# 32 of the 384 dense tokens of a PEER block take their first products from gathered rows of u

## The chip, the cores and the metric

The program runs on one core of one Trainium2 chip. The metric is device time in microseconds (us) of one execution; lower is better. Everything is fp32, and the large products are each split into three fp32r matmuls (a high and a low part of both operands, without low times low).

## The reference

One encoder layer over 512 tokens of width 1024: a norm, one input projection, attention and an HGRN2 recurrence side by side, a merge, then the part that matters here, PEER retrieval over 16384 one-neuron experts, and last a gated input embedding. The PEER part, cut:

```python
q = (ht @ w_q).reshape(T, 8, 2, 128)
s = einsum('thpc,hpnc->thpn', q, sub_keys)       # scores of 128 row keys and 128 column keys
v1, i1 = top_k(s[:, :, 0], 16);  v2, i2 = top_k(s[:, :, 1], 16)
top_s, pos = top_k(all 256 sums v1 + v2, 16)     # 8 heads x 16 = 128 slots for each token
idx = i1 * 128 + i2 of the chosen;  g = softmax(top_s)
a = einsum('thkd,td->thk', u[idx], x);  w = gelu(a) * g
out = einsum('thk,thkd->td', w, v[idx])
```

## The kernel before

The 512 tokens stand in four blocks of 128. Block 0 (tokens 0 to 127) is **gathered**: for each of its 128 slots one row of u per token comes by an indirect DMA that GpSimd issues (`slot_u`, tile `gu`, 128 rows of 4 KB), VectorE multiplies it with `h2n` and sums it into one column of `aa` (L889); after gelu and the gate (`slot_w`) a row of v follows (`slot_v`, tile `gv`), which VectorE adds into `acc` (L898).

The other 384 tokens (blocks 1 to 3, `TD`) are **dense**: all 16384 experts are computed for them, in 128 chunks of 128 experts. For a chunk `dense_a` loads u (`u_raw`), splits it (`u_h` on ScalarE, `u_l` on VectorE, L139 and L140), and TensorE makes `pa` with 24 matmuls (8 slices of the width, 3 products each, L134 to L136) of 384 columns; ScalarE writes gelu of it to `ge`. The gate table G, which is zero but for the 128 slots of a token, is built in blocks of 32 tokens (`build`, 4 for each token block, 12 in all): one-hot rows `gE` on VectorE, `gR` on ScalarE, a matmul `pg` for each token, and a store of the block to DRAM (`gdram`). For a chunk `w_prep` loads its v rows (`v_raw`, split into `v_h` and `v_l`) and every fourth time a piece of G (`gchg`), multiplies `ge` by G (L1002), and splits the product (`w_h`, `w_l`). Then 18 matmuls of 512 columns add to `po` (3 token blocks, 2 halves, 3 products).

This gives three stages after the query products end at 606 us. **Stage A** (to 1016.7 us, where the first `po` matmul starts): the top-16 choice of each block (`sel`) and the building of G, and beside it the dense chunks at a pace of one for every `APACE` units of a hand-set cost. G is not yet there, so `ge` of the first `SP` chunks is parked in DRAM (`adram`) and read back later (`ges`); `PRE` buffers hold `ge` of the others. Gathers of u start when the cost passes `GSTART` and go on at `GPACE`, from cost 135 on at `GPACE` + `GP2`. The whole cost of the units is 161.4 in both kernels. **Stage B**, 128 iterations `it`: `w_prep`, a fresh dense chunk where one is due, 18 `po` matmuls, and some gathers of u and v; the last `LASTN` = 4 iterations run token block by token block. At `it` = `IT1` = 118 the buffers of the u side are given up, and the embedding part loads its operands (the residual `x`, `pr`) and makes `pj`. **The tail**: residual, norm (`norm_T1`, transposes `pt_n`), and 16 gates of 24 matmuls each (`gate`, tile `pg`, 256 columns).

Each engine takes its instructions in the order in which a scheduler wrote them; the SyncE queue issues all loads and stores but the gathers, also in order, and waits there for a free buffer. The indirect gathers stand in GpSimd's queue. There are 4 `gu` and 4 `gv` buffers, 3 `v_raw`, 3 `u_raw`, 4 each of `v_h`, `v_l`, `w_h`, `w_l` and `ges`.

Of the kernel before, what the change touches and what calls it, by code (L numbers as in the profile page):

```python
# [8 lines left out]
F32 = mybir.dt.float32  # L9
# [19 lines left out]
C_ID, C_IOTA, C_COS, C_SIN, C_RST = 0, 128, 256, 384, 512  # L29
# [19 lines left out]
PRE = 8  # L49
SP = 62  # L50
TQ = 8
APACE = 2.6
# [7 lines left out]
IT1 = 118  # L60
WLAG = 4
# [6 lines left out]
G0 = 8  # L68
# [17 lines left out]
def const_arrays():  # L86
    c = np.zeros((128, C_END), np.float32)
# [18 lines left out]
    return c, m  # L106
# [19 lines left out]
def body(nc, tc, I, out, taps=None, stop=99):  # L126
# [17 lines left out]
    with contextlib.ExitStack() as top:  # L144
        glob = top.enter_context(tc.tile_pool(name="glob", bufs=1))
        cst = glob.tile([128, C_END], F32, name="cst")
# [49 lines left out]
        if True:  # L196
# [4 lines left out]
            hT_l = fp.tile([128, ND, T], F32R, name="hT_l")  # L201
            ysp = [[fp.tile([128, 4, T], F32R, name=f"{nm}{p}") for p in "hl"] for nm in "oy"]
# [11 lines left out]
            with tc.tile_pool(name="n1", side="right", bufs=1) as n1:  # L214
# [4 lines left out]
                DM.dma_start(cst[:, 0:C_COS], I["cst"][:, 0:C_COS])  # L219
# [7 lines left out]
                DM.dma_start(cst[:, C_COS:C_END], I["cst"][:, C_COS:C_END])  # L227
# [105 lines left out]
            def hgrn_head(h):  # L333
# [5 lines left out]
                V.tensor_tensor_scan(SC.rearrange(fl), cst[:, C_RST:C_END], LF.rearrange(fl), 0.0, OP.mult, OP.add)  # L339
# [144 lines left out]
            for tb in range(NT):  # L484
                for (src, dst, H, o, gg) in ((aq[:, tb, :], qr, 8, 0, qn_g), (akv[:, tb, 0:128], kr, 2, 8, kn_g)):
# [7 lines left out]
                    co, si = [cst[:, off + 32 * tb:off + 32 * tb + 32].rearrange("p (a i) -> p a i", a=2)[:, None]  # L493
# [159 lines left out]
        v8s = [pp.tile([128, 16, 16], F32, name=f"v8_{tb}") for tb in range(NT)]  # L653
        i8s = [pp.tile([128, 16, 16], U32, name=f"i8_{tb}") for tb in range(NT)]
        with s5:
# [49 lines left out]
            ul_st = contextlib.ExitStack()  # L705
            up = [ul_st.enter_context(tc.tile_pool(name="ustr0", side="left", **LR))]
# [50 lines left out]
def peer(nc, tc, I, out, xd, cst, gains, norm_T1, rstd_of, split, mm3, tap, stop, pp, ha, la, h2n, v8s, i8s, st, top,  # L757
# [8 lines left out]
    if True:  # L766
# [83 lines left out]
        def build(kp, bp, ps, tb, i_f, g_o):  # L850
# [3 lines left out]
            tij = kp.tile([128, 2, 128], F32, name="tij", tag="tij")  # L854
            S.activation(tij, pt[:, 0:2, :], AF.Copy)
            gr = kp.tile([128, 128], F32, name="gr", tag="gr")
            S.activation(gr, pt[:, 2, :], AF.Copy)
            for b in range(128 // GB):
# [59 lines left out]
        with s7:  # L918
# [42 lines left out]
            for u in units():  # L961
# [4 lines left out]
                if cost > GSTART:  # L966
                    gathers((cost - GSTART) * GPACE + max(0.0, cost - GS2) * GP2, None)
# [7 lines left out]

        vp = ys.enter_context(tc.tile_pool(name="vstr", side="right", bufs=2, reuse_waits="tile"))
# [4 lines left out]
        N0 = na  # L981
        def w_prep(it):
            c = it
# [12 lines left out]
            if spilled:  # L996
                ge = vp.tile([128, TD], F32, name="ges", tag="ges", bufs=B_GE)
                DM.dma_start(ge, ad[spidx[c]])
# [18 lines left out]
        for it in range(128):  # L1017
# [9 lines left out]
            if it < IT1:  # L1027
                if it >= G0:
                    gathers(GW + (it + 1 - G0) * (128 + WLAG - GW) / (IT1 - UEND - G0), VLEAD + (it + 1 - G0) * 128 / (IT1 - G0), ops[0], ops[5])
            if it == IT1:  # L1030
                gathers(999, 999, ops[0], ops[5])
# [8 lines left out]
                with tc.tile_pool(name="ple1a", side="left", **LR) as pa:  # L1040
# [7 lines left out]
                    for n in range(2):  # L1048
# [6 lines left out]
                        for tb in range(NT):  # L1055
                            sl = slice(tb * 128, (tb + 1) * 128)
                            pj = ps1.tile([128, 512], F32, name="pjp", tag="p1")
                            for k in range(2):
                                mm3(pj, ph[:, k, sl], pl[:, k, sl], jh[:, k, :], jl[:, k, :], k == 0, k == 1)
                            S.activation(PJ[tb][:, 512 * n:512 * n + 512], pj, AF.Copy)  # L1060
                V.tensor_tensor(X[0], X[0], acc, op=OP.add)
# [27 lines left out]
                norm_T1(pe2[0], ps1, "p1", X[0], 2, h3h, h3l, "n3", 0, B_XN)  # L1089
                gate(0, 0, *wg0, ps1, "p1")  # L1090
        for tb in range(3):
# [17 lines left out]
def layouts(a):  # L1109
    f = np.ascontiguousarray  # L1110
    c, m = const_arrays()
# [8 lines left out]
    for lo, hi, n in W_IN_TILES:  # L1120
# [24 lines left out]
        "cmask": m,  # L1145
    }
# [17 lines left out]
```

## Time and profile before

| | us |
|---|---|
| median of 3 runs (1858.29 to 1859.44) | 1858.76 |
| the profiled execution, own time | 1863.17 |
| its span in the trace | 1861.4 |
| TensorE busy | 1803.0 (97%) |
| VectorE busy | 1403.1 (75%) |
| ScalarE busy | 902.2 (48%) |
| GpSimd busy | 352.2 (19%) |

The span is what the trace's clock shows from the first to the last instruction. Busy time of TensorE counts matmuls whose ends are modelled and overlap, so what one matmul takes in a stream is read from the starts of two that follow each other. The granted clock is at its full level (2.4 GHz) in nearly all slices.

### The profile page before, as it was taken

The numbers are of one execution on the slowest core, as the hardware profiler recorded it, in microseconds if no ns is written. First come the engines' busy times: TensorE is split into PE (matmuls) and PEld (weight loads), VectorE is DVE, ScalarE is ACT, GpSimd is POOL, SyncE is SP. The second block draws the span as 40 slices with busy tenths as digits, with TensorE's granted clock in tenths as the row PEclk, the third lists the DMA queues.
The fourth block names the chain that finished last, engine by engine and source line by source line (L and its number), as shares of the span: only waits on it lengthen the run. The fifth ranks groups of instructions, "written<-read, shape, count | busy, mean of one in ns | idle before, by whom it ended". The sixth has DMA issues, their size and how long they took to land.

```text
span 1861.4 us, 27255 instructions
## 1 busy us (share of the span) xinstructions
PE 1803.0 (97%) x9989; PEld 1612.1 (87%) x9989; DVE 1403.1 (75%) x2844; ACT 902.2 (48%) x1561; POOL 352.2 (19%) x260
## 2 busy tenths in 40 slices
PE   6999999999999899998999999999999999999998
PEld 5997878888888899998999888888888888888888
DVE  3689776636599999997764888787777778766564
ACT  5745656542433557875696433333333333333442
POOL 0000000000000033333300244344343334321000
PEclk9999999999999999999999999999999999999999
DMA  4212100323321488887857999999999999987612
GB/s 163 83 46 80 58 13 12 122 92 126 146 82 56 142 315 305 298 300 280 329 186 260 359 360 352 316 344 320 336 328 320 314 335 325 312 268 219 208 60 88
DMA packets 162805, 402.95 MB, mean 216 GB/s; under 512 B 13552, under 2 KB 80880, under 8 KB 161008
## 3 DMA queue, kind: packets, MB, share of 16 engines
q1 hardware_dynamic: 125808, 266.98, 41.9%
q0 software_dynamic: 36864, 134.23, 20.2%
q8 instruction: 78, 1.28, 0.3%
q14 instruction: 55, 0.45, 0.1%
HBM read 359.62 MB, written 41.55 MB: 216 GB/s over the span
## 4 chain that ended last, share of the span: by engine, by line
PE 79%; DVE 10%; DMA 4%; ACT 3%; issue 2%; POOL 0%; SPq 0%; ACTq 0%; POOLq 0%; DVEq 0%
PE po L136 9%; PE po L135 9%; PE po L134 9%; PE pa L136 6%; PE pa L135 6%; PE pa L134 6%; PE pT L135 3%; PE pT L134 3%; PE pT L136 3%; PE pg L872 3%; DMA gdram<-gs 2%; PE poa L566 2%; PE pq L135 2%; PE pq L134 2%; PE pq L136 2%
## 5 line engine op out<-in xcount | busy, mean ns | idle before, releaser
L883 POOL DMA_INDIRECT gu<-in_peer_u_dram,idxg x128 | 196.6, 1536 | 1170.5 <-DVE cd L808 646.0
L136 PE MATMUL pa<-ha,u_l 128*128 128x384 f32 x1024 | 348.1, 340 | 11.9 <-DVE u_l L140 11.9
L134 PE MATMUL pa<-ha,u_h 128*128 128x384 f32 x1024 | 349.7, 342 | 1.8 <-ACT u_h L139 1.8
L135 PE MATMUL pa<-la,u_h 128*128 128x384 f32 x1024 | 346.9, 339 | 0.0
L136 PE MATMUL po<-v_h,w_l 128*128 128x512 f32 x768 | 299.9, 391 | 0.1
L135 PE MATMUL po<-v_l,w_h 128*128 128x512 f32 x768 | 300.0, 391 | 0.0
L134 PE MATMUL po<-v_h,w_h 128*128 128x512 f32 x768 | 298.8, 389 | 0.8 <-ACT w_h L139 0.8
L139 ACT ACTIVATE u_h<-u_raw 128x1024 fp32r<-128x1024 f32 x128 | 135.4, 1057 | 214.9 <-PE pa L135 114.0
L136 PEld LDWEIGHTS pa<-ha,u_l 128*128 128x128 f32 x1024 | 193.8, 189 | 14.8 <-DVE u_l L140 14.6
L140 DVE TENSOR_TENSOR u_l<-u_raw,u_h 128x1024 fp32r<-128x1024 f32 x128 | 156.3, 1221 | 63.2 <-ACT u_h L139 63.2
L134 PEld LDWEIGHTS pa<-ha,u_h 128*128 128x128 f32 x1024 | 194.0, 189 | 5.0 <-ACT u_h L139 2.6
L135 PEld LDWEIGHTS pa<-la,u_h 128*128 128x128 f32 x1024 | 193.8, 189 | 2.4
L883 POOL DMA_INDIRECT gv<-in_peer_v_dram,idxg x128 | 155.3, 1213 | 184.1 <-DVE acc L898 161.2
L995 DVE TENSOR_TENSOR v_l<-v_raw,v_h 128x1024 fp32r<-128x1024 f32 x128 | 156.5, 1223 | 39.3 <-ACT v_h L994 38.6
L136 PEld LDWEIGHTS po<-v_h,w_l 128*128 128x128 f32 x768 | 144.1, 188 | 30.7 <-DVE w_l L140 0.7
L134 PEld LDWEIGHTS po<-v_h,w_h 128*128 128x128 f32 x768 | 144.2, 188 | 29.6 <-ACT w_h L139 1.1
L135 PEld LDWEIGHTS po<-v_l,w_h 128*128 128x128 f32 x768 | 144.1, 188 | 28.8
L889 DVE SCALAR_TENSOR_TENSOR gu<-gu,h2n 128x1024 f32<-128x1024 f32 x128 | 155.5, 1219 | 13.4 <-DMA gu<-in_peer_u_dram,idxg 13.4
L898 DVE SCALAR_TENSOR_TENSOR acc<-gv,aa,acc 128x1024 f32<-128x1024 f32 x128 | 164.1, 1282 | 0.4 <-DMA gv<-in_peer_v_dram,idxg 0.2
L994 ACT ACTIVATE v_h<-v_raw 128x1024 fp32r<-128x1024 f32 x128 | 134.2, 1049 | 44.0 <-PE po L136 27.9
L867 ACT ACTIVATE gR<-gE,gr 128x128 f32<-128x128 f32 x384 | 122.2, 394 | 33.1 <-DVE gE L864 32.9
L864 DVE TENSOR_TENSOR gE<-cst,tij 128x2048 f32<-128x2048 f32 x48 | 109.3, 2287 | 17.0 <-PE pg L872 17.0
(321 smaller groups left out, 3341.3 us busy)
## 6 DMA issues: line engine op xcount, KB each, us to landing
u_raw<-in_u_t_dram SPq DMA_DIRECT2D x128, 512.0 KB
v_raw<-in_peer_v_dram SPq DMA_DIRECT2D x128, 512.0 KB
gdram<-gs SPq DMA_DIRECT2D x12, 2048.0 KB
gchg<-gdram SPq DMA_DIRECT2D x32, 768.0 KB
w_raw<-in_w_in_dram SPq DMA_DIRECT2D x42, 512.0 KB
adram<-ge SPq DMA_DIRECT2D x62, 192.0 KB
ges<-adram SPq DMA_DIRECT2D x62, 192.0 KB
wq_raw<-in_peer_wq_dram SPq DMA_DIRECT2D x16, 512.0 KB
```

What stands on the lines that cost most here:

```text
L134: PE.matmul(ps, lh, rh, start=first, stop=False)
L135: PE.matmul(ps, lh, rl, start=False, stop=False)
L136: PE.matmul(ps, ll, rh, start=False, stop=last)
L139: ins = S.activation(hi, raw, AF.Copy)
L140: V.tensor_tensor(lo, raw, hi.bitcast(F32), op=OP.subtract)
L864: V.tensor_tensor(EE, iota[:, None, None, :].to_broadcast([128, 2, TQ, 128]), tij[:, :, t0:t0 + TQ, None].to_broadcast([128, 2, TQ, 128]), ...
L867: S.activation(RR[:, t, :], EE[:, 1, t, :], AF.Copy, scale=gr[:, t0 + t:t0 + t + 1])
L883: G.indirect_dma_start(out=t, out_offset=None, in_=src, in_offset=bass.IndirectOffsetOnAxis(ap=idxg[:, k:k + 1], axis=0))
L889: V.scalar_tensor_tensor(t, t, 1.0, h2n, op0=OP.mult, op1=OP.mult, accum_out=aa[:, k:k + 1])
L898: V.scalar_tensor_tensor(acc, t, aa[:, k:k + 1], acc, op0=OP.mult, op1=OP.add)
L994: S.activation(vh, vr, AF.Copy)
L995: vi.append(V.tensor_tensor(vl, vr, vh.bitcast(F32), op=OP.subtract))
```

## The change

Tokens 128 to 159, the first 32 of the dense ones (`RC` = 32), no longer go through `pa`: a chunk's 24 matmuls have 352 columns, and `ge` holds ones in the first 32. Their first products come from rows of u, laid out anew: 32 tokens times 128 slots are 32 gathers of 128 rows, with 4 groups of 32 slots on the partitions. `rows_h` makes the tokens' vectors for this layout (`hC`), `rows_idx` the indices and gates, `row_u` gathers and multiplies, and `rows_w` puts gelu times gate into `gr`, from which the first block of G is then built, last of all blocks instead of first. Since `ge` is one there, the G table carries the finished weights.

Besides: block 1 is chosen before block 0; `SP` goes from 62 to 66, `PRE` from 8 to 7, `APACE` from 2.6 to 2.44; the paced number of u gathers now counts the 32 new ones first. In stage B the u gathers spread to `it` = 118 (before: 110), those of v to 128 (before: 118), from a pool of their own that outlives the u side; the rest of block 0 (adding `acc`, norm, first gate) moves from `it` = 118 to behind the first token block's last matmuls. The read-back of `ges` is issued ahead of `gchg` and `v_raw`, and `pj` is made at `it` = 123. Some constants and the top-8 lists move to other pools.

```diff
-PRE = 8
-SP = 62
+RC = 32
+PRE = 7
+SP = 66
-APACE = 2.6
+APACE = 2.44
+VEND = 128
 def dense_a(c):
-                mm3(pa, uh[:, e], ul[:, e], ha[:, k, NG:T], la[:, k, NG:T], k == 0, k == ND - 1)
+                mm3(pa[:, RC:], uh[:, e], ul[:, e], ha[:, k, NG + RC:T], la[:, k, NG + RC:T], k == 0, k == ND - 1)
-                S.activation(ge, pa, AF.Gelu_apprx_tanh)
+                S.activation(ge[:, RC:], pa[:, RC:], AF.Gelu_apprx_tanh)
+                S.activation(ge[:, 0:RC], ones, AF.Copy)
+            def rows_h():
+                hs = kp.tile([128, D], F32, name="hs")
+                for dst in (hs, hC):
+                    for half in range(2):
+                        pt = ps.tile([128, 128, 4], F32, name="pg", tag="pg").rearrange("p i t -> p (i t)")
+                        if dst is hs:
+                            for j in range(4):
+                                k = 4 * half + j
+                                for n, h in enumerate((ha, la)):
+                                    PE.matmul(pt[:, j * 128:(j + 1) * 128], h[:, k, NG:NG + 128].bitcast(F32), ident, ...)
+                        else:
+                            PE.matmul(pt, csel[:, 0, :], hs[:, 512 * half:512 * half + 512], start=True, stop=True)
+                        S.activation(dst[:, 512 * half:512 * half + 512], pt, AF.Copy)
+            def rows_idx(i_f, g_o):
+                V.scalar_tensor_tensor(x, i_f[:, 0, :], 128.0, i_f[:, 1, :], op0=OP.mult, op1=OP.add)
+                PE.matmul(pt[:, 0, :], csel[:, 0, :], x, start=True, stop=True)
+                PE.matmul(pt[:, 1, :], csel[:, 0, :], g_o, start=True, stop=True)
...
+            def row_u(k):
+                t = gather(un, k, "gu", idxC)
+                V.scalar_tensor_tensor(t, t, 1.0, hC, op0=OP.mult, op1=OP.mult, accum_out=aC[:, k:k + 1])
+            def rows_w(gr):
+                S.activation(aC, aC, AF.Gelu_apprx_tanh)
+                V.tensor_tensor(aC, aC, gC, op=OP.mult)
...
+                PE.matmul(pt[:, 0, 0:RC], Z, csel[:, 2, 0:RC], start=True, stop=True)
+                S.activation(gr[:, 0:RC], pt[:, 0, 0:RC], AF.Copy)
             def units():
-                yield from sel(0)
-                yield from sel(1)
+                rows_h()
+                yield from sel(TB0)
+                rows_idx(*sels[TB0])
+                yield from sel(0)
                 for tb in (1, 2, 3):
-                    gens = [build(kp, bp, ps, tb, *sels[tb])]
+                    gens = [build(bp, ps, tb, *tg, range(1 if tb == TB0 else 0, 128 // GB))]
...
+                rows_w(first[1])
+                yield from build(bp, ps, TB0, *first, [0])
                 if cost > GSTART:
-                    gathers((cost - GSTART) * GPACE + max(0.0, cost - GS2) * GP2, None)
+                    want = int((cost - GSTART) * GPACE + max(0.0, cost - GS2) * GP2)
+                    while rows["ok"] and rows["n"] < min(RC, want):
+                        row_u(rows["n"])
+                        rows["n"] += 1
+                    gathers(want - RC, None)
-            if it < IT1:
-                if it >= G0:
-                    gathers(GW + (it + 1 - G0) * (128 + WLAG - GW) / (IT1 - UEND - G0), VLEAD + (it + 1 - G0) * 128 / (IT1 - G0), ops[0], ops[5])
+            if it >= G0:
+                gathers(999 if it >= IT1 else GW + (it + 1 - G0) * (128 + WLAG - GW) / (IT1 - G0), (it + 1 - G0) * 128 / (VEND - G0), ops[0], ops[5])
             if it == IT1:
-                gathers(999, 999, ops[0], ops[5])
                 ul_st.close()
```

In the queue of GpSimd, before, the gathers of u of block 0 (`idxg`) come first, with a few of v between them, and those of v follow:

```order
L883 DMA gu<-in_peer_u_dram,idxg 128x1024 x4
L883 DMA gv<-in_peer_v_dram,idxg 128x1024
L883 DMA gu<-in_peer_u_dram,idxg 128x1024 x4
L883 DMA gv<-in_peer_v_dram,idxg 128x1024 x3
L883 DMA gu<-in_peer_u_dram,idxg 128x1024 x55
L883 DMA gv<-in_peer_v_dram,idxg 128x1024 x2
```

At the same place of the changed kernel the 32 gathers of the new rows (`idxC`) lead:

```order
L902 DMA gu<-in_peer_u_dram,idxC 128x1024 x32
L902 DMA gu<-in_peer_u_dram,idxg 128x1024 x29
L902 DMA gv<-in_peer_v_dram,idxg 128x1024 x4
L902 DMA gu<-in_peer_u_dram,idxg 128x1024
L902 DMA gv<-in_peer_v_dram,idxg 128x1024
```

Before the first gather of v is used, block 0 has thus some 29 rows of u where it had some 63; the missing ones move into stage B.

On VectorE, before, from the split of v of `it` = 12 on, what stage B does for two iterations (`ges` and `ge` are multiplied by G, `gu` and `acc` are gather steps):

```order
L995 TENSOR_TENSOR v_l<-v_raw,v_h 128x1024
L1002 TENSOR_TENSOR ges<-ges,gchg 128x384
L889 SCALAR_TENSOR_TENSOR gu,aa<-gu,h2n 128x1024
L995 TENSOR_TENSOR v_l<-v_raw,v_h 128x1024 x2
L1002 TENSOR_TENSOR ges<-ges,gchg 128x384
L140 TENSOR_TENSOR u_l<-u_raw,u_h 128x1024
L1002 TENSOR_TENSOR ge<-ge,gchg 128x384
L889 SCALAR_TENSOR_TENSOR gu,aa<-gu,h2n 128x1024
L140 TENSOR_TENSOR w_l<-ge,w_h 128x384
L898 SCALAR_TENSOR_TENSOR acc<-gv,aa,acc 128x1024
L140 TENSOR_TENSOR w_l<-ges,w_h 128x384
```

The same place of the changed kernel:

```order
L1094 TENSOR_TENSOR v_l<-v_raw,v_h 128x1024
L1100 TENSOR_TENSOR ges<-ges,gchg 128x384
L908 SCALAR_TENSOR_TENSOR gu,aa<-gu,h2n 128x1024
L148 TENSOR_TENSOR w_l<-ges,w_h 128x384
L917 SCALAR_TENSOR_TENSOR acc<-gv,aa,acc 128x1024
L1094 TENSOR_TENSOR v_l<-v_raw,v_h 128x1024
L1100 TENSOR_TENSOR ge<-ge,gchg 128x384
L908 SCALAR_TENSOR_TENSOR gu,aa<-gu,h2n 128x1024
L148 TENSOR_TENSOR w_l<-ge,w_h 128x384
L917 SCALAR_TENSOR_TENSOR acc<-gv,aa,acc 128x1024
```

Each iteration now has one gather step of u and one of v, and a `w_l` stands behind one split of v where two splits of v and one of u stood ahead of it. On TensorE the scheduler puts 73.2 chunks of `pa` ahead of the first `po` (before: 68.4), the first fresh chunk comes after 13 iterations of `po` (before: 11), and `pj` after 124 (before: 119).

On SyncE, in the changed kernel, the loads of the end of stage B stand so (`x` is the residual, `pr` the embedding's operands, `wg_r` the first gate weights):

```order
L1090 DMA v_raw<-in_peer_v_dram 128x1024 x2
L1135 DMA x_0_16137<-xdram 128x1024
L1135 DMA x_1_16138<-xdram 128x1024
L1135 DMA x_2_16139<-xdram 128x1024
L1135 DMA x_3_16140<-xdram 128x1024
L1090 DMA v_raw<-in_peer_v_dram 128x1024
L1088 DMA gchg<-gdram 128x12x128
L1080 DMA ges<-adram 128x384
L1090 DMA v_raw<-in_peer_v_dram 128x1024
L1142 DMA pr<-in_pT_dram 128x1024
```

The order of the first five is that of before; ten loads of v follow behind `x`, where eight did, and the gathers of v now run beside them to the end.

## Rows read from the trace of the kernel before

**Rows 1.** The page: busy shares, then clock, DMA and GB/s in 40 slices.

```profile
PE 1803.0 (97%) x9989; PEld 1612.1 (87%) x9989; DVE 1403.1 (75%) x2844; ACT 902.2 (48%) x1561; POOL 352.2 (19%) x260
...
PEclk9999999999999999999999999999999999999999
DMA  4212100323321488887857999999999999987612
GB/s 163 83 46 80 58 13 12 122 92 126 146 82 56 142 315 305 298 300 280 329 186 260 359 360 352 316 344 320 336 328 320 314 335 325 312 268 219 208 60 88
```

**Rows 2.** Busy by stretch: start:end, length, then each engine, clock, DMA share, GB/s.

```profile
606.00:692.00 86.00, 78.56 (x432) 75.26 (x430) 82.54 (x347) 45.48 (x55) 18.91 (x15) 0.96 0.67 236
692.00:1016.70 324.70, 308.73 (x1997) 301.79 (x1996) 260.84 (x406) 244.78 (x594) 81.65 (x51) 0.99 0.77 278
1016.70:1100.00 83.30, 83.16 (x385) 70.94 (x386) 70.38 (x97) 34.74 (x52) 29.77 (x21) 1.00 1.00 354
1100.00:1600.00 500.00, 500.00 (x2443) 444.22 (x2442) 395.38 (x490) 179.38 (x251) 195.34 (x148) 1.00 0.94 330
1600.00:1700.00 100.00, 100.00 (x491) 88.95 (x491) 74.01 (x87) 35.30 (x50) 25.35 (x20) 1.00 0.82 269
1700.00:1755.00 55.00, 55.00 (x260) 47.63 (x259) 32.58 (x39) 20.03 (x27) 0.94 (x1) 1.00 0.68 223
1755.00:1809.40 54.40, 53.03 (x252) 43.71 (x252) 30.83 (x76) 25.39 (x46) 0.00 (x0) 1.00 0.26 81
```

**Rows 3.** Waits of TensorE in stage B, to 1809 us: all there are.

```profile
PE pjp L134 <- ACT pj L1060: 0.9, 1, 0.9
PE po L134 <- ACT w_h L139: 0.8, 1, 0.8
PE pt_n L184 <- DVE xn_n L179: 0.5, 2, 0.3
```

**Rows 4.** Waits of the SyncE queue, 1100 to 1700 us.

```profile
SPq L991 <- DVE v_l L995: 215.6, 87, 5.2
SPq L713 <- DVE u_l L140: 171.2, 52, 3.8
```

**Rows 5.** Waits of ScalarE, 1100 to 1700 us: operands made ahead wait for TensorE.

```profile
ACT w_h L139 <- PE po L135: 149.8, 61, 2.7
```

**Rows 6.** Waits of TensorE in stage A, 606 to 692 us, then to 1016 us.

```profile
PE pa L136 <- DVE u_l L140: 5.6, 6, 3.2
PE pa L134 <- ACT u_h L139: 1.8, 2, 1.5
...
PE pa L136 <- DVE u_l L140: 6.3, 3, 4.6
PE pg L872 <- ACT gs L874: 5.2, 5, 2.1
```

**Rows 7.** Timeline of TensorE: a chunk's first matmul, the next 18 `po`, two gate matmuls.

```profile
1693.04 0.33 PE L134 MATMUL pa<-ha,u_h 128*128 128x384 f32 x1
...
1697.22 0.39 PE L134 MATMUL po<-v_h,w_h 128*128 128x512 f32 x1
...
1701.34 0.33 PE L134 MATMUL pa<-ha,u_h 128*128 128x384 f32 x1
...
1839.78 0.28 PE L134 MATMUL pg<-wg_h,ha 128*128 128x256 f32 x1
1839.90 0.28 PE L135 MATMUL pg<-wg_l,ha 128*128 128x256 f32 x1
```

**Rows 8.** The same view, 128-column matmuls of the table build, merged.

```profile
969.99 3.23 PE L872 MATMUL pg<-gE,gR 128*128 128x128 f32 x26
```

**Rows 9.** Groups of VectorE by shape, 606 to 692 us: the splits of u.

```profile
L140 DVE TENSOR_TENSOR u_l<-u_raw,u_h 128x1024 fp32r<-128x1024 f32 x17 | 20.6, 1213 | 0.6 <-ACT u_h L139 0.6
```

**Rows 10.** The page's groups: line, engine, names, count, busy us, mean ns.

```profile
L140 DVE TENSOR_TENSOR u_l<-u_raw,u_h 128x1024 fp32r<-128x1024 f32 x128 | 156.3, 1221 | 63.2 <-ACT u_h L139 63.2
L889 DVE SCALAR_TENSOR_TENSOR gu<-gu,h2n 128x1024 f32<-128x1024 f32 x128 | 155.5, 1219 | 13.4 <-DMA gu<-in_peer_u_dram,idxg 13.4
...
L874 ACT ACTIVATE gs<-pg 128x512 f32<-128x512 f32 x96 | 55.4, 590 | 16.0 <-DMA gdram<-gs 10.7 <-PE pg L872 4.1 <-issue 0.8
```

**Rows 11.** The DMA view: the gathers' queue, then issues with their count and KB each.

```profile
q0 software_dynamic: 36864, 134.23, 20.2%
...
gchg<-gdram SPq DMA_DIRECT2D x32, 768.0 KB
...
ges<-adram SPq DMA_DIRECT2D x62, 192.0 KB
```

**Rows 12.** The same view, 1100 to 1600 us: GB/s in slices of 12.5 us.

```profile
GB/s 375 316 370 362 335 307 366 314 289 362 367 302 363 319 360 234 360 328 330 333 346 312 288 381 296 284 340 369 297 342 276 342 313 369 307 343 302 331 344 337
```

More of the change, by code (lines that the diff above doesn't have):

```diff
@@ L60 @@
 IT1 = 118
+VEND = 128
+GLEAD = 0
 WLAG = 4
@@ L705, in body @@
             ul_st = contextlib.ExitStack()
+            tp = ul_st.enter_context(tc.tile_pool(name="top8", side="left", **LR))
+            v8s = [tp.tile([128, 16, 16], F32, name=f"v8_{tb}") for tb in range(NT)]
+            i8s = [tp.tile([128, 16, 16], U32, name=f"i8_{tb}") for tb in range(NT)]
             up = [ul_st.enter_context(tc.tile_pool(name="ustr0", side="left", **LR))]
@@ L853, in build @@
                 PE.transpose(pt[:, i, :], s, ident)
-            tij = kp.tile([128, 2, 128], F32, name="tij", tag="tij")
+            tij = kp.tile([128, 2, 128], F32, name="tij", tag="tij" + c)
             S.activation(tij, pt[:, 0:2, :], AF.Copy)
-            gr = kp.tile([128, 128], F32, name="gr", tag="gr")
+            gr = kp.tile([128, 128], F32, name="gr", tag="gr" + c)
             S.activation(gr, pt[:, 2, :], AF.Copy)
-            for b in range(128 // GB):
+            return tij, gr
+        def build(bp, ps, tb, tij, gr, blocks):
+            for b in blocks:
                 gs = bp.tile([128, 128, GB], F32, name="gs", tag="gs", bufs=1)
@@ L946, in units @@
                     yield from zipped(*gens)
+                while rows["n"] < RC:
+                    row_u(rows["n"])
+                    rows["n"] += 1
+                rows_w(first[1])
+                yield from build(bp, ps, TB0, *first, [0])
             na, cost = 0, 0.0
@@ L981, in peer @@
         N0 = na
+        back = {}
+        nb = 0
         def w_prep(it):
+            nonlocal nb
+            while nb < min(128, it + 1 + GLEAD):
+                if nb in spidx:
+                    back[nb] = vp.tile([128, TD], F32, name="ges", tag="ges", bufs=B_GE)
+                    DM.dma_start(back[nb], ad[spidx[nb]])
+                nb += 1
             c = it
@@ L996, in w_prep @@
             if spilled:
[L997 to L998 removed]
+                ge = back.pop(c)
             else:
@@ L1039, in peer @@
                     DM.dma_start(X[tb], xd[tb])
-                with tc.tile_pool(name="ple1a", side="left", **LR) as pa:
+                ple = contextlib.ExitStack()
+                pa = ple.enter_context(tc.tile_pool(name="ple1a", side="left", **LR))
+                if True:
+                    jw = []
                     raw = pa.tile([128, D], F32, name="pr", tag="pr", bufs=2)
@@ L1054, in peer @@
                         split(r3, jh, jl)
[L1055 to L1061, printed above, removed]
+                        jw.append((jh, jl))
+            if it == IT1 + 5:
+                for n, (jh, jl) in enumerate(jw):
+                    for tb in range(NT):
+                        sl = slice(tb * 128, (tb + 1) * 128)
+                        pj = ps1.tile([128, 512], F32, name="pjp", tag="p1")
+                        for k in range(2):
+                            mm3(pj, ph[:, k, sl], pl[:, k, sl], jh[:, k, :], jl[:, k, :], k == 0, k == 1)
+                        S.activation(PJ[tb][:, 512 * n:512 * n + 512], pj, AF.Copy)
+                ple.close()
                 pe2 = [e1.enter_context(tc.tile_pool(name="ple2", side="left", **LR))]
@@ L1097, in peer @@
             norm_T1(pe2[0], ps1, "p1", X[tb + TB0], 2, h3h, h3l, "n3", tb + TB0, B_XN)
+            if tb == 0:
+                gathers(999, 999)
+                V.tensor_tensor(X[0], X[0], acc, op=OP.add)
+                norm_T1(pe2[0], ps1, "p1", X[0], 2, h3h, h3l, "n3", 0, B_XN)
+                gate(TB0, 0, *wg0, ps1, "p1")
         ys.close()
@@ L1103, in peer @@
                 w = wg0 if n == 0 else load_wg(n)
-                for tb in range(1 if n == 0 else 0, NT):
+                for tb in (0, 2, 3) if n == 0 else range(NT):
                     gate(tb, n, *w, ps, "pg2")
```

76 lines of the change are left out of this document (57 added, 19 removed).

## The prediction

> **What bounds the kernel now.** I read the page first: TensorE is busy 97% of the span, VectorE 75%, and DMA stands at 9 tenths from the middle on [rows 1]. A mean over stages says little, so the busy time by stretch comes next [rows 2]. In stage B (from 1016.7 us) TensorE is busy without a break; its waits to 1809 us are 0.9 + 0.8 + 0.5 = 2.2 us in all [rows 3]. There each matmul removed is time removed, as long as nothing else becomes late. The reader should note two neighbours in the same rows: DMA at a share of 1.00 and 354 GB/s up to 1100 us, then 0.94 and 330 GB/s for 500 us, and VectorE at 395.38 / 500 = 79%. Operands are nevertheless early: the loads of v and u in SyncE's queue wait for VectorE to free a buffer (87 and 52 times, 387 us together) [rows 4], and ScalarE waits 149.8 us for TensorE to free a `w_h` buffer [rows 5]. Four buffers ahead is about four iterations.
>
> Stage A is mixed. In its first 86 us VectorE is busy 82.54 (96%), TensorE only 78.56, and TensorE waits for `u_l` there [rows 2, 6]; then TensorE has 308.73 of 324.7 us (95%) and VectorE 80%, with 16 us of TensorE's gaps.
>
> **The width: the gain.** What a matmul costs in a stream is the distance of starts: 24 of `pa` take 1697.22 - 1693.04 = 4.18 us, 0.174 each at 384 columns; 18 of `po` take 1701.34 - 1697.22 = 4.12, 0.229 each at 512; two gate matmuls stand 0.12 apart at 256 [rows 7]. The steps 256 to 384 and 384 to 512 are 0.054 and 0.055, 0.42 ns a column on both sides, so 352 columns cost 0.174 - 32 x 0.00042 = 0.1605. The row that bounds it from the other side is that of 128 columns: 26 in 3.23 us [rows 8], at most 0.124, where the line would give 0.066; a floor is there, but below 256. So 3072 matmuls x 0.0135 = **41.5 us less**, a chunk 0.324 less (3.85).
>
> **What of it is lost in stage A.** In the first 86 us 17 chunks run [rows 9], and VectorE sets the pace: their 17 x 0.324 = 5.5 is not won; I count -5 (bounds 0 and -5.5). With 73.2 chunks ahead of the first `po` instead of 68.4, TensorE has 73.2 x 3.85 = 282 us of them instead of 286, while VectorE gets 4.8 more splits of u, 4.8 x 1.22 [rows 10] = 5.9. The 32 row steps don't add to it: each is one such step of 1.219 [rows 10] as those of block 0 that they push out (57 instead of 58 gathers are paced in stage A). Folding indices and gates is half a dozen VectorE steps on 128 columns. As VectorE has 20% to spare behind the first 86 us, I count 2 for all this (0 to 8).
>
> **New work on TensorE.** `rows_h` has 16 matmuls of 128 columns, `rows_idx` two and `rows_w` one: 19 x 0.12 = 2.3. Two of 512 columns in plain fp32 have no row; the bounds are 0.229 (the split kind) and four times that, 0.5 to 1.8 for both. Copies out of PSUM stand between them on ScalarE, four of 0.59 by the copy of `pg` [rows 10], and dense matmuls stand between in the order. I take 4 for all (2.8 to 7). `rows_w` is a short chain ahead of the last block of G, and nine to forty `pa` matmuls separate its pieces: nothing, and 3 if it stands bare. ScalarE's copy of ones for each chunk is ScalarE work at 179 of 500 us [rows 2]: nothing.
>
> **Stage B: what DMA has to carry.** A gather is 134.23 MB / 256 = 0.524 MB [rows 11], and so is a load of v or u; `gchg` is 0.786 every fourth iteration, `ges` 0.197 in half of them [rows 11]. Of block 0, 58 rows of u were done at the start of stage B; now it is 57 - 32 = 25. From `it` = 8 the code asks for (132 - 25) / 110 = 0.973 of u and 128 / 120 = 1.067 of v an iteration (before 0.725 and 1.164); with one v and 62 / 114 = 0.544 fresh chunks that is 3.584 x 0.524 + 0.197 + 0.101 = 2.18 MB. TensorE's time for it is 4.12 + 0.544 x 3.85 = 6.21 us, so **351 GB/s** are needed, where the same sum for before gives 2.11 MB in 6.54, 322 (measured: 330). The rows bound what can be had: 354 over 83 us at a share of 1.00, and single slices of 370 to 381 [rows 2, 12]. The stream therefore just fits, with no room for recovery. I count nothing for it on average, and -2 for the start, where 13 iterations of `po` alone run (before 11) and the last five of them ask for 1.89 MB in 4.12 us, 459 GB/s: at 370 each falls 1 us behind, 5 us against the lead of four buffers; bound 8. At the end 11 iterations of `po` alone ask for 1.38 MB each, and the embedding's 3.7 MB come beside them: 18.9 MB in 45 us, 51 at 370 GB/s, so 6 late, against the same lead: nothing (bound 8).
>
> The Trainium skill speaks against the change here: "DMA: Bandwidth & Descriptors", Specifications, gives about 358 GB/s as a core's share of HBM. The trace has slices of 381 above it [rows 12], and the skill's "Perfetto Trace Analysis" (Roofline) says that a lone core can draw more. With 358 as a ceiling the 351 would still pass and the first stretch would fall 1.2 us behind in each of the five iterations instead of 1.0.
>
> VectorE in stage B, an iteration: one `v_l`, 0.544 `u_l`, 0.973 and 1.067 gather steps of 1.2 to 1.3, two half-size steps: 3.58 x 1.22 + 1.1 = 5.5 by row means of 6.21 us. It is not the bound, but there are 14% more gather steps in a us (2.04 in 6.21 against 1.89 in 6.54), and each that lands late blocks the splits behind it.
>
> **The tail.** The first gate of block 0 (24 x 0.12 = 2.9 us) was inside TensorE's full stretch and now stands behind it, so its place is worth nothing; the norm of block 0 moves between the norms of the others, on ScalarE and VectorE that are half idle there (30.83 of 54.4 [rows 2]). I count -1 (0 to 6). It needs the last gathers of v, which are asked for up to `it` = 127.
>
> **The sum.** 41.5 - 5 - 2 - 4 - 2 - 1 = 27.5 us less. The profiled execution took 1863.2 (span 1861.4 and 1.8 around it), 4.4 over the median of the runs, so the same sum gives 1836 there and **1831** against the median of 1858.8. With the gentle bounds (0, 0, 2.8, 0, 0) it is -38.7, 1820 (some of stage A's 16 us of gaps closing might give 2 more); with the harsh ones (5.5, 8, 10, 16, 6) it turns to +4, 1863.
>
> **Rivals.**
> - *DMA carries no more than in the long stretch before, 330 GB/s.* 2.18 / 0.330 = 6.60 instead of 6.21, over iterations 14 to 112: 99 x 0.39 = 39 us late, **1870, slower**. For: that is the only long measured rate. Against: it was what was asked for (322), the share was 0.94, and 354 is shown. It decides at the rate where 99 x (2.18 / r - 6.21) = 27.5, r = 336. Chance 0.08.
> - *In between, 342 GB/s,* 6.37 an iteration, 16 us late: **1847**. Chance 0.10.
> - *Stage A keeps the chunk's old pace*, since VectorE's order, not TensorE, sets it. 4.8 more chunks in it at 410 / 68.4 = 6.0 us are 29 us longer; stage B wins 59.6 x 4.18 - 54.8 x 3.85 = 38, less 3: -6, **1853**. For: 96% in the first 86 us and the waits for `u_l`. Against: 80% afterwards. Chance 0.08.
> - *A matmul of 352 columns costs as one of 384*: no gain, 14 us of extras, **1873**. Against: three points on one line [rows 7]. Chance 0.02.
>
> The forecast, 15 to 41 us less, has 0.72. A measurement of this kernel can tell about 0.2%, 3.7 us, from no change. Faster: 0.72, 0.10, and most of 0.08 for stage A: 0.87. Same: 0.04. Slower: 0.09. The range, **1818 to 1850**, reaches over the middle rival and leaves out those over 1850 (0.18); the forecast's own is 1818 to 1844.
>
> **What the changed profile would show.** The width: `pa` starts 0.16 apart, and 24 in about 3.85. Stage A: the first `po` at 1020 to 1026 us. DMA: a share of 0.98 to 1.00 and 345 to 360 GB/s between 1100 and 1650 us, loads of v that still wait for VectorE and not the other way round; wrong if TensorE has gaps in stage B that end with `w_h`, `v_h` or `u_l` behind a DMA or a gather. The end of `po` about 34 us before the old 1809. The prediction is wrong if a 352-column matmul is not 0.16, if the first `po` comes after 1035, or if TensorE's idle time in stage B passes 15 us.

## The result, and the profile after

The changed kernel takes **1835.9 us** (median of 4 runs, 1834.2 to 1837.3), the kernel before 1859.1 beside it: a ratio of 0.9871 (95% interval 0.9856 to 0.9886), about 24 us less. The forecast was 1831 (1818 to 1850), so the sign and the range were right and the gain was put about 4 us too high. The profiled execution has a span of 1835.4 against 1861.4 [rows 1], 26.0 less; the account below is made on these two.

The page of the changed kernel: span, shares, DMA and GB/s in 40 slices, the gathers' queue.

```profile
span 1835.4 us, 27579 instructions
PE 1769.8 (96%) x10031; PEld 1578.7 (86%) x10031; DVE 1434.9 (78%) x2917; ACT 915.1 (50%) x1695; POOL 409.6 (22%) x292
DMA  5212100324431368798965999999999999998921
GB/s 168 81 47 81 56 14 13 115 92 131 160 104 58 100 210 299 266 329 296 346 242 191 316 360 392 387 393 358 352 353 367 355 351 346 353 362 266 329 78 67
q0 software_dynamic: 41472, 151.01, 22.5%
```

Busy time by stretch, as in [rows 2]; stage A now ends at 1029.9, stage B at 1779.2.

```profile
606.00:692.00 86.00, 76.27 (x454) 73.12 (x453) 77.12 (x315) 49.48 (x81) 11.95 (x9) 0.96 0.56 181
692.00:1029.90 337.90, 315.48 (x2109) 308.40 (x2108) 268.58 (x436) 253.70 (x652) 84.58 (x57) 0.97 0.80 286
1029.90:1100.00 70.10, 69.13 (x300) 57.19 (x301) 55.51 (x76) 26.30 (x39) 20.38 (x16) 0.96 0.92 328
1100.00:1600.00 500.00, 500.00 (x2519) 442.03 (x2519) 432.96 (x561) 191.18 (x310) 245.42 (x172) 1.00 1.00 364
1600.00:1700.00 100.00, 100.00 (x503) 88.16 (x502) 80.07 (x102) 36.65 (x60) 36.96 (x28) 1.00 0.92 319
1700.00:1779.20 79.20, 79.20 (x364) 66.07 (x363) 59.91 (x95) 36.12 (x56) 10.14 (x8) 1.00 0.65 223
1779.20:1835.40 56.20, 50.95 (x404) 48.79 (x404) 29.13 (x82) 19.50 (x46) 0.00 (x0) 0.99 0.17 58
```

Read it against [rows 2] from the bottom up. Stage B is 749.3 us instead of 792.7, with TensorE full and DMA at 364 GB/s over 500 us, where 351 were thought to be needed. Stage A went the other way: the first `po` starts 13.2 us later. TensorE's idle time there is 9.7 + 22.4 = 32.1 us, 8.7 more than 7.4 + 16.0 before. And the granted clock, the third column from the right, is lower: 0.04 x 86 + 0.03 x 337.9 + 0.04 x 70.1 = 16 us of full clock are missing, against 0.04 x 86 + 0.01 x 324.7 = 7 before. (The clock has two decimals, so such sums are good to some 2 us; and they count a low clock also where TensorE stands idle, where it costs nothing more.)

The timeline of TensorE gives the new width: the first and the last two `pa` of a chunk, then the first `po`.

```profile
1641.74 0.33 PE L142 MATMUL pa<-ha,u_h 128*128 128x352 f32 x1
1645.24 0.32 PE L143 MATMUL pa<-la,u_h 128*128 128x352 f32 x1
1645.40 0.32 PE L144 MATMUL pa<-ha,u_l 128*128 128x352 f32 x1
1645.56 0.39 PE L142 MATMUL po<-v_h,w_h 128*128 128x512 f32 x1
```

24 starts in 1645.56 - 1641.74 = 3.82 us are 0.159 each. The one wait of TensorE over half a microsecond within stage B is 1.0 us; in stage A, with the first `po`, they are these (columns as in [rows 6]):

```profile
PE pg L889 <- ACT gs L891: 11.1, 4, 4.7
PE pa L144 <- DVE u_l L148: 10.7, 6, 6.0
PE po L142 <- ACT v_h L1093: 4.4, 1, 4.4
PE pg L889 <- ACT gR L884: 4.1, 4, 1.9
```

The third is new: a gap of 4.45 us between the last `pa` and the first `po`. The chain that ended last, and the timeline, show how it comes about (SPq is SyncE's queue; start, length, line, names, and the idle time with what ended it).

```profile
1007.74 11.00 DMA gdram<-gs
...
1019.24 9.53 DMA v_raw<-in_peer_v_dram
```

```profile
1018.81 0.38 SPq L1088 DMA_DIRECT2D gchg<-gdram  x1
1019.24 1.99 SPq L1090 DMA_DIRECT2D v_raw<-in_peer_v_dram  x1
...
1027.58 0.56 DVE L1100 TENSOR_TENSOR ges<-ges,gchg 128x384 f32<-128x384 f32 x1 [3.85 <-DMA gchg<-gdram]
1028.17 0.52 ACT L147 ACTIVATE w_h<-ges 128x384 fp32r<-128x384 f32 x1 [5.23 <-DVE ges L1100]
...
1028.80 1.06 ACT L1093 ACTIVATE v_h<-v_raw 128x1024 fp32r<-128x1024 f32 x1
```

The store of G's last block takes 11.0 us. The load of G is issued when it has landed, and the first load of `v`, queued behind that, takes another 9.5. And the gap costs more than itself. The same stretch in windows (columns as in [rows 2]):

```profile
1026.00:1030.00 4.00, 0.10 (x1) 0.10 (x1) 1.23 (x3) 1.73 (x3) 0.00 (x0) 0.85 1.04 397
1030.00:1032.00 2.00, 2.00 (x5) 1.61 (x6) 2.00 (x3) 2.00 (x4) 0.00 (x0) 0.50 0.40 150
1032.00:1034.00 2.00, 2.00 (x6) 1.52 (x6) 2.00 (x3) 1.45 (x3) 0.00 (x0) 0.50 0.81 225
1034.00:1036.00 2.00, 2.00 (x7) 1.56 (x6) 2.00 (x4) 1.18 (x2) 0.00 (x0) 0.59 1.03 316
1036.00:1038.00 2.00, 2.00 (x11) 1.62 (x10) 2.00 (x4) 0.82 (x2) 0.00 (x0) 1.00 1.11 370
```

While TensorE stands still the granted clock falls to 0.50, the level of 1.2 GHz, and it stays there till about 1035: five to seven matmuls fall into 2 us instead of 11. The time counts as busy, so the page's 96% hides it.

### The profile page after: what moved, and what is told of

Read it like the earlier page. It is cut to its first block, busy times and chain, and to the rows that moved or that the text cites. A ratio compares the mean times of both kernels' runs of the same rounds, so it can differ in the third digit from the quotient of the medians.

```text
span 1835.4 us, 27579 instructions
## 1 busy us (share of the span) xinstructions
PE 1769.8 (96%) x10031; PEld 1578.7 (86%) x10031; DVE 1434.9 (78%) x2917; ACT 915.1 (50%) x1695; POOL 409.6 (22%) x292
## 4 chain that ended last, share of the span: by engine, by line
PE 81%; DVE 8%; DMA 6%; ACT 3%; issue 1%; SPq 0%; POOL 0%; ACTq 0%; DVEq 0%; POOLq 0%
PE po L142 9%; PE po L143 9%; PE po L144 9%; PE pa L144 7%; PE pa L142 6%; PE pa L143 6%; PE pg L889 4%; PE pT L142 3%; PE pT L143 3%; PE pT L144 3%; DMA v_raw<-in_peer_v_dram 2%; DMA gdram<-gs 2%; PE poa L575 2%; PE pq L142 2%; PE pq L143 2%; PE pq L144 2%
## 5 line engine op out<-in xcount | busy, mean ns | idle before, releaser
L144 PE MATMUL pa<-ha,u_l 128*128 128x352 f32 x1024 | 336.1, 328 | 10.9 <-DVE u_l L148 10.7
L142 PE MATMUL pa<-ha,u_h 128*128 128x352 f32 x1024 | 337.3, 329 | 0.9 <-ACT u_h L147 0.9
L143 PE MATMUL pa<-la,u_h 128*128 128x352 f32 x1024 | 333.2, 325 | 0.0
L902 POOL DMA_INDIRECT gu<-in_peer_u_dram,idxg x128 | 204.8, 1600 | 367.9 <-DVE gu L908 345.9
L902 POOL DMA_INDIRECT gu<-in_peer_u_dram,idxC x32 | 45.7, 1429 | 760.8 <-ACT u_h L147 650.7
```

Source lines behind the costliest of these rows:

```text
L142: PE.matmul(ps, lh, rh, start=first, stop=False)
L143: PE.matmul(ps, lh, rl, start=False, stop=False)
L144: PE.matmul(ps, ll, rh, start=False, stop=last)
L902: G.indirect_dma_start(out=t, out_offset=None, in_=src, in_offset=bass.IndirectOffsetOnAxis(ap=idx[:, k:k + 1], axis=0))
```

## The experiments

Each ran beside the kernel before. In short (us; the ratio is to the kernel before):

| run | us | ratio (95% interval) |
|---|---|---|
| the change | 1835.9 | 0.9871 (0.9856 to 0.9886) |
| 352 columns alone, no rows | 1818.1 | 0.9774 (0.9759 to 0.9789) |
| the change at 384 columns | 1867.3 | 1.0042 (1.0027 to 1.0058) |
| without `rows_h` on TensorE | 1829.6 | 0.9829 (0.9813 to 0.9846) |
| `v` ahead of G in the queue | 1833.1 | 0.9868 (0.9853 to 0.9884) |
| 67 parked chunks | 1845.1 | 0.9926 (0.9913 to 0.9940) |
| 62 parked chunks, 2.6 a chunk | 1825.9 | 0.9810 (0.9791 to 0.9828) |
| tokens through DRAM, `v` first | **1812.5** | 0.9749 (0.9733 to 0.9765) |
| the same, 62 and 2.6 | 1818.1 | 0.9772 (0.9756 to 0.9789) |
| old place of the first gate | 1833.3 | 0.9863 (0.9838 to 0.9889) |
| extra loads | 1834.5 | 0.9855 (0.9838 to 0.9871) |
| 64 tokens by rows | 1814.6 | 0.9748 (0.9732 to 0.9764) |
| 64 tokens, through DRAM, `v` first | 1821.8 | 0.9804 (0.9785 to 0.9823) |

**The width alone**, on the kernel before:

```diff
-    mm3(pa, uh[:, e], ul[:, e], ha[:, k, NG:T], la[:, k, NG:T], k == 0, k == ND - 1)
+    mm3(pa[:, RC:], uh[:, e], ul[:, e], ha[:, k, NG + RC:T], la[:, k, NG + RC:T], k == 0, k == ND - 1)
-    S.activation(ge, pa, AF.Gelu_apprx_tanh)
+    S.activation(ge[:, RC:], pa[:, RC:], AF.Gelu_apprx_tanh)
+    S.activation(ge[:, 0:RC], ones, AF.Copy)
```

> The kernel before with the first products of 352 of the 384 dense columns; the first 32 get a 1 in place of the gelu and nothing takes their first products, so their rows of the result are left wrong; queues, pacing and gathers are those of before. Theory (the gain is the width alone, 3072 x 0.0135 = 41.5 us, of which what VectorE sets in the first part of stage A is lost): 33 to 41 us less than before, 1818 to 1826. Rival (the gain rests on the new numbers of parked chunks and pacing and on the new order of the gathers): less than 20 us, above 1839. Second rival (matmuls of 352 columns gain less than their line says): also above 1830, with pa further apart than 0.161.

42 us less than before, and 18 less than the change. So the gain is the width, and all else that the change brings costs about 18. Stage A, busy time as above:

```profile
606.00:692.00 86.00, 76.47 (x444) 74.09 (x444) 81.33 (x328) 48.46 (x77) 16.96 (x14) 0.92 0.67 235
692.00:1002.50 310.50, 300.48 (x2022) 293.82 (x2022) 262.86 (x425) 250.02 (x644) 91.54 (x52) 0.98 0.81 292
```

In the first 86 us, where VectorE is still at 95%, the width won next to nothing: by 692 us ScalarE had made `ge` of 17 chunks, as before, TensorE's idle time was 9.5 us instead of 7.4, and 0.08 x 86 = 7 us of clock were missing instead of 3. That agrees with the -5 of the prediction, though more of it is clock than waits. Behind it the idle time fell from 16.0 to 10.0, so all of stage A has 19.5, less than before. Its missing clock is 0.08 x 86 + 0.02 x 310.5 = 13, some 6 more than before. The width at its measured worth (48, below) less 6, and 4 less idle, makes 46, where this execution, the slowest of its four, is 43 shorter than that of before; 3 stay open.

**The change at full width:**

```diff
-    mm3(pa[:, RC:], uh[:, e], ul[:, e], ha[:, k, NG + RC:T], la[:, k, NG + RC:T], k == 0, k == ND - 1)
+    mm3(pa, uh[:, e], ul[:, e], ha[:, k, NG:T], la[:, k, NG:T], k == 0, k == ND - 1)
```

> The changed kernel with its first products over all 384 columns again (the 32 extra columns are computed and thrown away); all else as changed. Theory: the rest of the change is a pure cost of 12 to 18 us, so this run takes 1871 to 1877, 36 to 41 more than the changed kernel; DMA needs less per us and is below 1.00 in the long stretch. Rival (the new pacing brings part of the gain): at or below 1859.

Slower than before by 8 us (5 to 11): the rest of the change is a pure cost, and the rival is out. But it is a smaller one than the 12 to 18 expected and than under the narrow width, and the 32 columns are worth only 32 us here. Idle time in stage A was 23 us in this run, as before the change, where the narrow kernel has 32: beside the rest of the change, about 9 us of the width turn into waits in stage A. This is argued from one trace of each; in the run of the width alone the idle time did not grow. Some 5 to 7 us of the difference I can't assign.

**Without `rows_h` on TensorE:**

```diff
 def rows_h():
-    hs = kp.tile([128, D], F32, name="hs")
-    ...
+    DM.dma_start(hC, I["x"][128:256, :])
```

> The changed kernel without the 18 matmuls and four copies of rows_h: the tokens' vectors are loaded from x instead, so the values of the 32 tokens are wrong and the work behind them is the same. Theory (TensorE loses their time, 5 to 6 us of the first part of stage A): 4 to 6 us less than the changed kernel, 1830 to 1832. Rival (VectorE sets the pace there, so they are hidden): no difference, 1834 to 1838.

6 to 8 us less than the change: `rows_h` lies bare. Its rows in the changed kernel:

```profile
611.13 0.38 PE L975 MATMUL pg<-cst,ha 128*128 128x128 f32 x2
611.35 0.39 PE L975 MATMUL pg<-cst,la 128*128 128x128 f32 x2
...
615.20 1.13 PE L978 MATMUL pg<-hs,csel 128*128 128x512 f32 x2 [0.34 <-ACT hs L979]
615.76 0.72 PE L142 MATMUL pa<-ha,u_h 128*128 128x352 f32 x1
616.32 0.33 PE L143 MATMUL pa<-la,u_h 128*128 128x352 f32 x1
...
617.48 1.13 PE L978 MATMUL pg<-hs,csel 128*128 128x512 f32 x2 [0.34 <-ACT hs L979]
```

A plain fp32 matmul is recorded as two (x2). By starts it takes 0.22 us at 128 columns. At 512, one of them and a `pa` of 0.16 fill the 1.12 us from 615.20 to 616.32, so it takes 0.96, where an fp32r one of 512 takes 0.23 (the 1.13 in its row has a modelled end). That makes 16 x 0.22 + 2 x 0.96 = 5.4 us, and about 1 us of waits for ScalarE's copies.

**`v` ahead of G:**

```diff
 def w_prep(it):
+    vr = vp.tile([128, D], F32, name="v_raw", tag="v_raw", bufs=B_VR)
+    DM.dma_start(vr, vn[it * 128:(it + 1) * 128, :])
     (the loads of ges and gchg)
-    (the same two lines)
```

> The changed kernel with the load of v issued ahead of the loads of the parked chunk and of G in each iteration. Theory (v_raw stands in SyncE's queue behind the load of G, which waits for G's store; w_h is there at 1028.7, so only 1.2 us of the gap belong to v): the gap ahead of the first po falls from 4.45 to about 3.2 us, time 1 us less or not to be told from 1836. Rival (v alone holds the first po, the load of G comes sooner when it isn't waited behind): the gap falls under 1 us, 1832.

The gap became 1.3 us, ended by `w_h` (and 1.2 before the last chunk), the first `po` came at 1021.1, and the clock there stayed at 1.00. So the load of `v` seems to have held more of the gap than the theory gave it; in size the rival was nearer. In time it is 1 to 3 us, not to be told from none: its runs spread from 1825 to 1836, with a mean granted clock between 0.991 and 0.997, and the trace is of the fastest. Nor is the early first `po` the edit's alone, since the last store of G was issued at 999.1 us there and at 1007.7 in the change. The edit does what it should at its place; what stage A has besides in drops of the clock differs from run to run.

**One more parked chunk,** `SP = 67`:

> The changed kernel with one more parked chunk (67), so one more chunk of pa stands between the last block of G and the first po. Theory (the 4.45 us gap ahead of the first po is TensorE waiting for the store of G and the loads behind it, and a chunk of 3.85 us fills it): 3 to 4 us less than the changed kernel, 1832 to 1833, the gap down to about 0.6, the first po at the same time. Rival (the store and the loads move with the chunk, or the extra parked chunk costs what it saves in stage B): within 1.5 us of 1836.

Wrong on both counts: 9 to 10 us more than the change. The gap was still 3.0, and stage B had a new one of 8.2 us. The chain in order of time (start, length, what):

```profile
1065.74 15.50 DMA v_raw<-in_peer_v_dram
...
1081.34 1.06 ACT v_h L1093
...
1084.12 1.15 DVE gu L908 x2
...
1087.48 0.80 PE po L142
```

A load of `v` takes 15.5 us in the burst of loads that iterations of `po` alone ask for (404 GB/s from 1052 to 1072 us), and when it has been split, VectorE works till 1086.9 us through what stood behind its `v_l` (`ges`, a `gu` step, `u_l`, `ge`) before the next `w_h` can be made. That is the case for which the prediction had set the bound of 8 us at the start of stage B, one chunk further on. But the trace is of the fastest of five executions (1837.9), and the other four took 1845 to 1846; what their 7 us more are no trace shows.

**The old numbers:** `SP = 62`, `APACE = 2.6`, all else as changed.

> The changed kernel with 62 parked chunks and 2.6 a chunk as before, 7 chunks ahead as in the change. Theory (these numbers only move the same chunks between the stages): 1832 to 1840. Rival (they carry part of the gain): 1845 or more.

10 to 11 us *less* than the change. The gap ahead of the first `po` is 0.8 us, the clock there 1.00, and the missing clock of stage A 0.06 x 86 + 0.02 x 320.4 = 12:

```profile
606.00:692.00 86.00, 77.12 (x455) 73.73 (x455) 77.64 (x321) 50.52 (x86) 11.26 (x9) 0.94 0.54 178
692.00:1012.40 320.40, 301.10 (x2036) 293.27 (x2034) 264.64 (x429) 248.25 (x636) 91.13 (x57) 0.98 0.81 293
```

So the new numbers didn't carry the change, they took from it. (`PRE` stays 7 here: with 8 buffers the embedding's pool, 32 KB of a partition, finds only 31.125 free.)

**Tokens through DRAM, `v` first:** the normed rows are stored once and read back four times, so TensorE turns nothing back.

```diff
+    if tb == 1:
+        V.tensor_tensor(xn[0:RC], xn[0:RC], gf[0:RC], op=OP.mult)
+        DM.dma_start(I["hd"], xn[0:RC])
 ...
 def rows_h():
+    for s in range(0, 128, RC):
+        DM.dma_start(hC[s:s + RC], I["hd"])
```

> The same two edits on the changed kernel (32 tokens), with a right result. Theory (rows_h 6 us, v ahead of G 1 to 4 us with the drop of the clock behind the gap): 1825 to 1829. Rival (the two gains are one, time won in stage A is lost again in the gap ahead of the first po): 1829 to 1833.

1812.5, better than both expectations and the best of 32 tokens: 23 us less than the change, 47 less than before. Its windows:

```profile
606.00:692.00 86.00, 78.93 (x472) 75.66 (x471) 80.94 (x338) 48.34 (x76) 11.17 (x9) 0.98 0.60 196
692.00:1009.00 317.00, 304.90 (x2080) 298.34 (x2079) 267.83 (x429) 254.64 (x654) 89.06 (x56) 0.99 0.82 299
1009.00:1100.00 91.00, 91.00 (x425) 77.35 (x426) 78.45 (x108) 37.04 (x57) 34.04 (x26) 1.00 0.98 356
```

Idle time in stage A is 7.1 + 12.1 = 19 us instead of 32 and missing clock 5 instead of 16, 24 us together; 6 of TensorE's work are gone besides. (The products ahead of stage A ended some 4 us later in this execution than in that of the change, so not all of it shows in the end: the spans differ by 24.) The two edits alone brought 6 to 8 and at most 3. Together they also took away most of the other gaps and drops in stage A (waits for `gs` 3.9 us instead of 11.1). Behind a wait for `gs` stands the store of the block before, since `gs` has one buffer (ScalarE waited 12.4 us for these stores in the change, 6.2 here); why these waits went is not settled, for nothing in the edits touches that store. With 62 and 2.6 on top:

> The run at 1812.5 (32 tokens, vectors through DRAM, v ahead of G) with 62 parked chunks and 2.6 a chunk as before. Theory (the old numbers helped the changed kernel by 10 us because they closed the gap ahead of the first po and the drop of the clock behind it, and here both are gone already): 1809 to 1816, no difference to be told. Rival (the two gains add): 1800 to 1805. Second rival (with fewer gaps the clock drops elsewhere): 1818 or more at a granted clock under 0.995.

No gain but 4 to 6 us more, at a missing clock of 6 us. The time is that of the second rival, its reason is not: the granted clock was 0.996. What the old numbers had closed was closed already, and with fewer chunks parked stage B is longer, 758 us against 746, while the first `po` comes only 7 us sooner.

**The old place of the first gate:** `VEND = 118`, and block 0's sum, norm and first gate ahead of the last `po`.

> The changed kernel with the v rows asked for until iteration 118 as before, and the norm and the first gate of block 0 ahead of the last po again. Theory (the change pays 4.3 us in the tail for this move): the time behind the last po falls from 52.1 to 48 us, 1831 to 1833 in all, DMA at 1.00 carries the 359 GB/s that this asks for. Rival (the later end of the v rows is what keeps stage B free of waits): gaps of TensorE in stage B of 5 us or more, 1836 or more.

From the last `po` to TensorE's last matmul it is 46.0 us instead of 52.1, and stage B 754.6 instead of 749.3, so most of what leaves the tail comes back there. In time the move is not to be told from none, and DMA carried the denser stream at 372 GB/s between 1100 and 1600 us.

**Extra loads:**

```diff
+    if it % 4 == 1 and it < 114:
+        xl = lp.tile([128, D], F32, name="xl", tag="xl", bufs=1)
+        DM.dma_start(xl, vn[c * 128:(c + 1) * 128, :])
```

> The changed kernel with one more 512 KB load of v in every fourth iteration up to 113, into a buffer that nothing reads: 0.13 MB an iteration more, 364 + 21 = 385 GB/s in the long stretch of stage B. Theory (364 GB/s was what was asked for, the stretches of 383 to 393 show that more is to be had): under 5 us more than the changed kernel, up to 1841, and a share of 1.00 with 378 to 385 GB/s between 1100 and 1600 us. Rival (a share of 1.00 means that 364 is the ceiling): 0.36 us an iteration over 100 iterations less the lead, 30 us more, 1866, and TensorE gaps behind v_h or w_h all through stage B.

Inconclusive. Nothing reads these loads, so they were placed ahead of stage B, at 460 to 600 us, as the slices 11 to 13 show beside those of the change (160, 104 and 58 there):

```profile
GB/s 168 82 47 81 54 17 13 115 92 137 232 234 184 68 236 257 297 310 287 372 264 185 327 373 390 384 393 361 348 355 368 351 357 350 348 363 261 328 81 67
```

**64 tokens by rows:** `RC = 64`, and the last two blocks of G behind the rows.

> The changed kernel with 64 tokens by gathered rows instead of 32, so first products of 320 columns. It saves TensorE another 41 us and asks for 16.8 MB more; since rows take all the gathers that stage A can pace, the 128 rows of u of block 0 fall into stage B: about 2.27 MB in 5.9 us, 386 GB/s, and VectorE at 97%. Theory (DMA and VectorE take over as the bound at about this point): no more to win, 1826 to 1850, with TensorE gaps in stage B. Rival (the recipe scales, TensorE is still the bound): 1795 to 1805. Second rival (a ceiling of 364 GB/s): 33 us late in stage B, 1850 or more.

21 to 23 us less than the change, which is more than the theory allowed and less than either bound of the rival. A chunk's first matmul and the first `po` behind its 24, then stage B between 1100 and 1600 us, then its waits of TensorE:

```profile
1303.42 0.30 PE L142 MATMUL pa<-ha,u_h 128*128 128x320 f32 x1
...
1306.93 0.39 PE L142 MATMUL po<-v_h,w_h 128*128 128x512 f32 x1
```

```profile
1100.00:1600.00 500.00, 492.48 (x2530) 430.07 (x2529) 451.15 (x595) 186.26 (x307) 257.55 (x195) 1.00 1.03 383
```

```profile
PE po L144 <- DVE w_l L148: 5.1, 6, 1.3
PE pjp L142 <- ACT pj L1162: 2.8, 1, 2.8
PE pa L144 <- DVE u_l L148: 2.2, 2, 1.3
```

The 24 take 3.51 us, 0.146 each. 383 GB/s over 500 us: the 364 of the change was what was asked for and no ceiling. VectorE is at 90%, and TensorE waits some 10 us in stage B, most of it for VectorE. The edits that gave 23 us at 32 tokens make this one slower:

> 64 tokens by rows (the run at 1814.6), their vectors not turned back by TensorE but written to DRAM after the norm of their block and read back in two copies, and the load of v issued ahead of the loads of the parked chunk and of G. Theory (rows_h costs TensorE 6 us of stage A and the hand-over another 1 to 4): 1804 to 1809. Rival (with 64 tokens VectorE or DMA sets the pace of stage A and of stage B, so TensorE's work there is hidden): 1812 to 1816.

1821.8. TensorE's idle time in stage A is 8.1 + 32.4 = 40 us (34 without the edits), at a clock of 0.94 and 0.96. Neither expectation had a loss in it. The rival was nearer: that the 6 us won from TensorE came back as gaps fits its view that TensorE isn't what sets stage A with 64 tokens. Why the gaps and the drops of the clock grew by more than that was not tested.

## Why the prediction was nearly right

Point by point, on the two profiled executions (26.0 us less):

| step | counted | measured |
|---|---|---|
| width | -41.5 | 3072 x (0.1745 - 0.1588) = -48 |
| stage A, VectorE and the rest | +5 +2 | idle +8.7, clock about +7: +15 |
| new work on TensorE | +4 | +6 |
| stage B, start | +2 | clock +3, no wait |
| tail | +1 | 56.2 for 52.0, less the gate's 2.9: +1.3 |

The two prices of a `pa` are means over the starts between 1130 and 1600 us. The sum makes -23. A further 3 us lie ahead of stage A, where the change touched nothing of this kind: in the execution before the clock dropped at 503 us, in the one after it didn't (first row before, second after).

```profile
503.00:509.00 6.00, 6.00 (x26) 5.43 (x25) 3.91 (x10) 3.56 (x9) 0.00 (x0) 0.55 0.01 3
503.00:509.00 6.00, 6.00 (x39) 5.33 (x38) 4.28 (x9) 4.77 (x10) 0.00 (x0) 1.00 0.17 33
```

- **The width** was the right mechanism, and the run of the width alone shows it. The size was short by 7: the line through 256, 384 and 512 columns made 0.0135 of 0.174 and 0.1605, where the rows have 0.1745 and 0.159. The steps from 384 to 352 and on to 320 (0.147 as the mean of the run of 64 tokens) are 0.016 and 0.012, not 0.0135 each.
- **"Stage A", -5 and -2,** is the term that failed in size: 15 measured for 7. The -5 held in the run of the width alone. In the change itself the first 86 us have 2.3 us more idle time than before, at the same clock. What went wrong is the -2 for everything behind them: 6.4 us more idle and some 7 us of clock. That is mainly the gap ahead of the first `po`, for which I had no term, longer waits for `gs`, and the clock behind them. The first `po` at 1029.9 was outside the 1020 to 1026 named for it, though inside the 1035 that would have made the forecast wrong.
- **"New work on TensorE", -4,** held in kind; it measures 6. The reading of [rows 8] was wrong: its 26 records are 13 matmuls, because the matmuls of the table build are plain fp32 too and recorded as two (768 records for 384 tokens). So one of 128 columns takes 0.22, not 0.12, which makes 16 x 0.1 = 1.6 us in `rows_h`, and the row shows no floor for the split matmuls of `pa`. Those of 512 columns lie just over the upper bound, 0.96 against four times 0.229.
- **"What DMA has to carry"**: right. 364 GB/s came where 351 were asked for by my sum (345 to 360 were named), at a share of 1.00, and TensorE had one wait of 1.0 us. The rivals at 330 and 342 GB/s are out. The Trainium skill ("DMA: Bandwidth & Descriptors", Specifications) gives about 358 as a core's share of HBM; the trace doesn't agree with it as a ceiling for this lone core, by 364 here and 383 with 64 tokens.
- **"The start" of stage B**, with its bound of 8, cost nothing, but the margin is one chunk: with 67 parked chunks the wait of 8 us was there.
- **The rival "stage A keeps the chunk's old pace"** (1853) was in part true. A chunk of stage A took 423.9 / 73.2 = 5.79 us after 410.7 / 68.4 = 6.00, where the full width would have made it about 5.62. But some 0.1 of what is missing is the new work, and with the width alone only the first 86 us kept the old pace. **"352 columns cost as 384"** is out.
- That the total came so close (26.0 on the profiled executions for 27.5) is in part luck: the gain of the width was counted 7 too small, the losses together 11 too small, and 3 came from ahead of stage A.

## What to carry to other kernels

Narrowing the matmul of an engine that is full pays about what its price in the rows says; count what the helpers put in its place on the same engine with prices of their own kind (plain fp32 is not fp32r, and one matmul can be two records). At a hand-over between two stages, look at the queue for a first load of the next stage that stands behind one that waits for the last store of the stage before. Here moving it closed most of that gap, though alone it gave no time that can be told from none. One more parked chunk cost 9 to 10 us, and four fewer with the old pace won about as much. Read the trace of a run beside the spread of its times: the traces of two runs here are of their fastest execution. Sum the missing clock by stretch beside the idle time, since it counts as busy.

## What the runs showed of the hardware

While TensorE stood still for the 4.45 us ahead of the first `po`, the granted clock of this lone core fell to 0.50 (1.2 GHz), and till it rose again some 3 us of full clock were missing, on top of the gap. Over the whole of stage A and the start of stage B that makes 16 us in the change and 5 in the best run; two versions that differ by 6 us in matmuls differ by 23 in time. DMA carried 383 and 387 GB/s over 500 us in the two runs of 64 tokens, at shares of 1.03.
